# A diffusion step on one core: the norm chains ranked 300 instructions further up in the planner's order

## The chip, the core and the metric

The kernel runs on one core of a Trainium2 chip. The core has five engines, each with its own queue that it works off strictly in order: TensorE (PE, whose weight loads the profile lists as PEld), VectorE (DVE), ScalarE (ACT), GpSimd (POOL) and SyncE (SP, which issues most transfers here). An instruction that waits holds up everything behind it in its own queue. The metric is device time in microseconds (us) of one execution; the kernel before is told by the median of 3 runs.

## The reference, cut to what matters

Two layers run over 1024 latent and 128 context tokens of width 1024. Each layer is

```
h = rmsnorm(x) * g * (1 + scale1) + shift1
x = x + gate1 * (concat(diff_attn(h), fourier(h), mla(h), gqa(h)) @ w_out)
h = rmsnorm(x) * g * (1 + scale2) + shift2
x = x + gate2 * (square(relu(h @ w1)) @ w2)
```

and the end is `y = rmsnorm(x) * g`, with `rmsnorm(x) = x * rsqrt(mean(x*x) + 1e-6)` over the 1024 channels of a token. So every token is normalised five times: before the mixer and before the MLP of each layer, and at the end.

## The kernel before, in words

Activations lie transposed: 8 tiles of 128 channels by 1152 tokens, and the tokens are worked in three blocks b = 0, 1, 2 of 384 (block 2 holds the last 256 latent and the 128 context tokens). One norm of one block therefore is: square each of 8 tiles on ACT (L531), add them up to one tile `acc` on POOL or DVE (L534, function `sq_add`), and then `norm_scale`. With five norms and three blocks it is called 15 times.

`norm_scale` (L538) is the chain that the change touches. **Sums:** three products of `acc` with a column of ones give the sum of squares of 3 x 128 tokens in a PSUM tile of the pool `psA` (six PE instructions `psA<-ones,pg`, as a float32 product is two). **Chain:** a DVE copy to SBUF (L548, `ss<-psA`), then `rstd`: DVE multiply and add (L323, `rv`), ACT square root (L327, `rs`), DVE reciprocal (L328, `ry`), and four DVE steps of one Newton iteration (L330, L333, L335, L338; the last writes `ro`). Each of these works on 128 x 3 elements. **Spread:** three products of `ro`, broadcast along a row, with the identity put 1/rms of each token on all 128 partitions, again in a `psA` tile (six PE instructions `psA<-ident,ro`). `psA` has two buffers.

The spread is then read by the tiles' multiplications on DVE: in `norm_h` (the norm before a mixer, L567 in layer 0, L570 in layer 1), in `norm_mlp` (L2003), and in `final` (L1958, followed by the store of the tile). In `norm_mlp` ACT then applies scale and shift (L2005), ACT writes the float16 high part (L306) and POOL, or DVE for one in four, the low part (L303); these parts feed the MLP's products, of which the first chunk (function `plain`) needs block 0, 1 and 2 in turn. In `norm_h` DVE writes the high part (L578) and DVE or POOL the low part (L303). DVE also adds every product of the output projection and of the MLP to x (L1685).

The order of the work has two makers. The program is written as Python generators, and `run` advances them in turn by weights; that gives each instruction its place in the program. Inside `norm_scale` one `yield PACE` between chain and spread lets another generator take a step in between. A planner then orders each engine's queue before the run: it plays the program through a model of the chip, and an engine that comes free takes, of the instructions whose inputs are ready in the model, the one of lowest rank. The rank is the place in the program; inside `with self.pri(n)` (which is `tc.high_priority(offset=n)`) the rank is n less. Before the change this is used for the output tiles of the attention (`YO_PRI`, 40) and for L1685 (`RE_PRI`, 60). The queue order is fixed by this plan, whatever the chip's real times are.

Of the kernel before, what the change touches and what calls it, by code (L numbers as in the profile page):

```python
# [21 lines left out]
D = 1024  # L22
# [48 lines left out]
P_NORM = 1  # L71
Y_ROT = 2

YO_PRI, RE_PRI = 40, 60

WL_DVE = (1, 1, 1)
XL_DVE = (0, 1, 2, 3)
# [126 lines left out]
class Kern:  # L204
# [334 lines left out]
    def norm_scale(self, b):  # L539

        nc = self.nc
        acc = self.acc.pop(b)
        p = self.ps("A")
        for j in range(3):
            self.mm(p[:, j:j + 1], acc[:, 128 * j:128 * j + 128], self.ones, True, True)
        self.free(acc)
        ss = self.sm([128, 3], "ss")
        nc.vector.tensor_copy(ss, p[:, 0:3])  # L548
        r = self.rstd(ss, 3, 1.0 / D)
        for _ in range(P_NORM):  # L550
            yield PACE
        pb = self.ps("A")
        for j in range(3):
            self.mm(pb[:, 128 * j:128 * j + 128], r[:, j:j + 1].to_broadcast([128, 128]), self.ident, True, True)
        return pb

    def norm_h(self, l, i, x, b, h, own=False):
# [1733 lines left out]
```

## Time and profile before

| | |
|---|---|
| median of 3 runs (lowest, highest) | 3426.4 us (3425.98, 3429.53) |
| profiled execution, its time | 3424.58 us |
| its span (first to last instruction) | 3422.5 us |
| busy PE, PEld | 3102.8 us (91%), 2225.8 us (65%) |
| busy DVE, ACT, POOL | 2271.7 (66%), 1594.7 (47%), 1453.2 us (42%) |
| chain that ended last, by engine | PE 58%, DVE 17%, DMA 8%, POOL 6%, issue 5%, ACT 5% |
| mean granted TensorE clock | 0.945 of 2.4 GHz |

A busy share is of the whole span. The stretches between the long phases matter here: output projection to MLP (about 940 to 1060 us in layer 0, 2615 to 2700 us in layer 1), MLP of layer 0 to mixer of layer 1 (1725 to 1800 us), and the end (3385 to 3422 us). In a row of the timeline, `[3.56 <-DVE ro L338]` says that the engine sat idle for 3.56 us before the row and that the end of that DVE instruction released it.

### The profile page before, as it was taken

The page shows a single profiled execution, that of the slowest core. Times are in us where ns is not written, and L with a number is a line of the kernel's source. Part 1 is how long each engine was busy: PE and PEld are TensorE (multiplying, and loading weights), DVE is VectorE, ACT ScalarE, POOL GpSimd, SP SyncE. Part 2 cuts the span into 40 slices and gives each one's busy share as a digit, 9 for nine tenths or more (in the row PEclk, how much of TensorE's full clock was granted, in tenths as well). Part 3 has the DMA queues.
Part 4 walks back from the last instruction along what each step waited for, and adds up shares of the span by engine and source line. Part 5 has one row for each costly group of instructions (what it writes and reads, how often), then busy time and mean ns, then how long its engine had stood idle before and what let it go on. Part 6 is the DMA issues. An engine that isn't in the chain of part 4 may idle for free.

```text
span 3422.5 us, 60243 instructions
## 1 busy us (share of the span) xinstructions
PE 3102.8 (91%) x23658; PEld 2225.8 (65%) x23658; DVE 2271.7 (66%) x5215; ACT 1594.7 (47%) x2594; POOL 1453.2 (42%) x1140
## 2 busy tenths in 40 slices
PE   7998788899978999999989978889999799999997
PEld 5887566677954555555578866667789455555554
DVE  6864565655387777777696565665444687777776
ACT  4432565667264334443343326567653544344432
POOL 1331366767454223232263226678654523222222
PEclk8999798999989999999999988899999899999998
DMA  6642444333312111111036433332341111111101
GB/s 221 200 153 84 125 152 153 97 97 103 114 38 74 43 33 62 42 46 50 15 136 200 143 93 124 128 114 71 108 157 44 50 44 44 49 47 47 50 25 56
DMA packets 140549, 310.86 MB, mean 91 GB/s; under 512 B 16613, under 2 KB 85682, under 8 KB 140266
## 3 DMA queue, kind: packets, MB, share of 16 engines
q1 hardware_dynamic: 134858, 300.85, 27.1%
q10 hardware_dynamic: 5408, 6.18, 0.5%
q8 instruction: 185, 3.03, 0.4%
q14 instruction: 98, 0.80, 0.1%
HBM read 233.87 MB, written 72.82 MB: 90 GB/s over the span
## 4 chain that ended last, share of the span: by engine, by line
PE 58%; DVE 17%; DMA 8%; POOL 6%; issue 5%; ACT 5%; SPq 0%; ACTq 0%; DVEq 0%; POOLq 0%
PE psD L281 38%; PE psA L281 9%; PE psB L281 6%; DVE pg L303 5%; POOL pg L303 5%; PE psC L281 4%; DMA pg<-in_ada_p 3%; DVE pg L1685 2%; DMA pg<-mqr 2%; ACT pg L306 2%; DVE mx L1327 1%; DMA pg<-in_dft_lat 1%; ACT pg L1819 1%; DVE wm L1745 1%; ACT pg L1822 1%
## 5 line engine op out<-in xcount | busy, mean ns | idle before, releaser
L281 PE MATMUL psD<-pg,pg 128*128 128x384 f16 (+6 forms) x10510 | 2029.7, 341 | 76.2 <-DVE pg L303 25.4
L303 POOL TENSOR_TENSOR pg<-pg,pg 128x1024 f16<-128x1024 f32 (+8 forms) x743 | 1190.3, 1616 | 1124.9 <-ACT pg L306 413.4
L281 PEld LDWEIGHTS <-pg 128*128 128x128 f16 x16056 | 1084.9, 100 | 771.8 <-issue 120.5
L303 DVE TENSOR_TENSOR pg<-pg,pg 128x512 f16<-128x512 f32 (+11 forms) x617 | 477.8, 795 | 265.0 <-ACT pg L306 249.8
L281 PEld LDWEIGHTS psD<-pg,pg 128*128 128x128 f32 x3576 | 613.2, 194 | 39.9 <-DVE pg L303 16.1
L306 ACT ACTIVATE pg<-pg 128x512 f16<-128x512 f32 (+8 forms) x777 | 431.2, 588 | 345.8 <-POOL pg L303 78.3
L281 PE MATMUL psA<-pg,pg 128*128 128x128 f16 (+7 forms) x2752 | 505.3, 295 | 87.4 <-DVE mx L1327 30.3
L1685 DVE SCALAR_TENSOR_TENSOR pg<-psD,gc,pg 128x384 f32<-128x384 f32 (+2 forms) x1024 | 473.4, 505 | 13.5 <-PE psD L281 13.3
L1327 DVE TENSOR_REDUCE mx<-psA 128x1 f32<-128x384 f32 x512 | 281.6, 555 | 212.9 <-PE psA L281 199.6
L1373 ACT ACTIVATE pg<-psB 128x1024 f32<-128x1024 f32 x320 | 301.5, 945 | 253.1 <-PE psB L281 219.7
L281 PEld LDWEIGHTS psA<-pg,pg 96*128 96x128 f32 (+2 forms) x1377 | 256.2, 209 | 149.4 <-DVE mx L1327 46.3
L281 PE MATMUL psB<-pg,pg 97*128 97x512 f32 (+3 forms) x1064 | 332.1, 428 | 18.3 <-ACT pg L1373 13.5
L281 PE MATMUL psC<-pg,pg 128*128 128x65 f16 (+1 forms) x7008 | 332.1, 201 | 9.7 <-POOL pg L303 8.2
L1380 ACT ACTIVATE pg<-pg 128x1024 f16<-128x1024 f32 x320 | 308.3, 980 | 35.8 <-DMA pg<-mk 13.8
L281 PEld LDWEIGHTS psB<-pg,pg 97*128 97x128 f32 (+3 forms) x1064 | 203.2, 207 | 50.8 <-ACT pg L1373 16.1
L281 PE MATMUL psD<-pg 128*128 128x384 f16 (+1 forms) x674 | 219.7, 328 | 8.3 <-DVE pg L303 4.8
L1332 DVE TENSOR_REDUCE mx<-psA 128x1 f32<-128x384 f32 x256 | 142.2, 556 | 100.4 <-PE psA L281 87.9
L1770 ACT ACTIVATE pg<-pg,wm 128x1024 f32<-128x1024 f32 x32 | 36.7, 1148 | 356.3 <-DVE wm L2042 356.1
L1785 POOL TENSOR_TENSOR pg<-pg 128x512 f32<-128x512 f32 x32 | 43.4, 1356 | 233.4 <-PE psA L281 181.6
L1751 POOL PARTITION_ALL_REDUCE wm<-wm x32 | 11.9, 373 | 277.7 <-DVE wm L1705 235.0
L531 ACT ACTIVATE pg<-pg 128x384 f32<-128x384 f32 x120 | 61.1, 520 | 143.1 <-DVE pg L1685 131.0
L306 ACT ACTIVATE pg<-psD 128x384 f32<-128x384 f32 (+3 forms) x104 | 54.4, 529 | 137.2 <-PE psD L281 132.1
(205 smaller groups left out, 2153.9 us busy)
## 6 DMA issues: line engine op xcount, KB each, us to landing
pg<-in_mlp_w SPq DMA_DIRECT2D x128, 512.0 KB
pg<-in_ada_p SPq DMA_DIRECT2D x96, 512.0 KB
pg<-in_w_out SPq DMA_DIRECT2D x16, 512.0 KB
pg<-y_dram SPq DMA_DIRECT2D x42, 192.0 KB
pg<-sk SPq DMA_DIRECT2D x16, 436.5 KB
sqp<-pg SPq DMA_DIRECT2D x36, 192.0 KB
mqp<-pg SPq DMA_DIRECT2D x36, 192.0 KB
pg<-sqp SPq DMA_DIRECT2D x16, 432.0 KB
```

Source lines behind the costliest of these rows:

```text
L281: self.nc.tensor.matmul(out, lhsT=lhsT, rhs=rhs, start=start, stop=stop, skip_group_check=skip)
L303: eng.tensor_tensor(out, a, b, ALU.subtract)
L306: self.nc.scalar.activation(out, in_, AF.Copy)
L531: self.nc.scalar.activation(q.t, x, AF.Square)
L1327: nc.vector.reduce_max(mx[:, t, i:i + 1], p[:, 0:TB], axis=AX.X)
L1332: nc.vector.reduce_max(mx[:, t, 2:3], p[:, 128:512], axis=AX.X)
L1373: nc.scalar.activation(e[:, 0:n], src, AF.Exp, scale=M["scale"])
L1380: nc.scalar.activation(pp[:, 0, 0:n], e[:, 0:n], AF.Copy)
L1685: self.nc.vector.scalar_tensor_tensor(xs, o(p), g, xs, op0=ALU.mult, op1=ALU.add)
L1745: nc.vector.reduce_max(m[:, i:i + 1], s[i].t, axis=AX.XY, apply_absolute_value=True)
L1770: nc.scalar.activation(v.t, v.t, AF.Identity, scale=sc)
L1785: nc.gpsimd.tensor_tensor(s1.t, a21, a22, ALU.add)
```

## The change

`norm_scale` wraps its sums with the chain, and then its spread, in `with self.pri(NRM_PRI)`, with `NRM_PRI = 300`. Nothing is computed in another way, no instruction is added or removed, and the place of every other instruction in the program stays. The multiplications that read the spread keep their rank.

```diff
-YO_PRI, RE_PRI = 40, 60
+YO_PRI, RE_PRI, NRM_PRI = 40, 60, 300
...
         acc = self.acc.pop(b)
-        p = self.ps("A")
-        for j in range(3):
-            self.mm(p[:, j:j + 1], acc[:, 128 * j:128 * j + 128], self.ones, True, True)
-        self.free(acc)
-        ss = self.sm([128, 3], "ss")
-        nc.vector.tensor_copy(ss, p[:, 0:3])
-        r = self.rstd(ss, 3, 1.0 / D)
+        with self.pri(NRM_PRI):
+            p = self.ps("A")
+            for j in range(3):
+                self.mm(p[:, j:j + 1], acc[:, 128 * j:128 * j + 128], self.ones, True, True)
+            self.free(acc)
+            ss = self.sm([128, 3], "ss")
+            nc.vector.tensor_copy(ss, p[:, 0:3])
+            r = self.rstd(ss, 3, 1.0 / D)
         for _ in range(P_NORM):
             yield PACE
-        pb = self.ps("A")
-        for j in range(3):
-            self.mm(pb[:, 128 * j:128 * j + 128], r[:, j:j + 1].to_broadcast([128, 128]), self.ident, True, True)
+        with self.pri(NRM_PRI):
+            pb = self.ps("A")
+            for j in range(3):
+                self.mm(pb[:, 128 * j:128 * j + 128], r[:, j:j + 1].to_broadcast([128, 128]), self.ident, True, True)
         return pb
```

## Rows read from the trace of the kernel before

**Rows 1.** Groups by line and form, whole span: busy, mean ns | idle before, releasers.
```profile
L281 PE MATMUL psA<-ident,ro 128*128 128x128 f32 x90 | 16.8, 335 | 25.5 <-DVE ro L338 15.5 <-DVE wm L1721 10.1
L281 PE MATMUL psA<-ones,pg 128*128 128x1 f32 x90 | 13.7, 268 | 10.0 <-DVE pg L534 5.1 <-POOL pg L534 4.9
```
**Rows 2.** Timeline, final norm of blocks 1 and 2: start, length, engine, line [idle].
```profile
3396.88 0.72 PE L281 MATMUL psA<-ones,pg 128*128 128x1 f32 x6
...
3403.35 0.15 DVE L548 COPY ss<-psA 128x3 f32<-128x3 f32 x1
3403.49 2.06 POOL L534 TENSOR_TENSOR pg<-pg,pg 128x384 f32<-128x384 f32 x2 [0.18 <-ACT pg L531]
...
3406.08 1.65 PE L281 MATMUL psA<-ident,ro 128*128 128x128 f32 x6 [4.55 <-DVE ro L338]
3407.52 1.28 PE L281 MATMUL psA<-ones,pg 128*128 128x1 f32 x6
...
3411.98 0.15 DVE L548 COPY ss<-psA 128x3 f32<-128x3 f32 x1
...
3413.51 1.62 PE L281 MATMUL psA<-ident,ro 128*128 128x128 f32 x6 [4.71 <-DVE ro L338]
3415.24 4.29 DVE L1958 SCALAR_TENSOR_TENSOR pg<-pg,cols,psA 128x384 f32<-128x384 f32 x8 [1.87 <-PE psA L281]
```
**Rows 3.** Timeline, layer 0's MLP norm, block 2 (and the end of block 1's).
```profile
976.29 0.73 PE L281 MATMUL psA<-ones,pg 128*128 128x1 f32 x6
...
977.87 3.32 DVE L2003 TENSOR_TENSOR pg<-pg,psA 128x384 f32<-128x384 f32 x7
...
981.11 0.15 DVE L548 COPY ss<-psA 128x3 f32<-128x3 f32 x1
...
992.11 0.19 ACT L327 ACTIVATE rs<-rv 128x3 f32<-128x3 f32 x1
...
993.40 1.62 PE L281 MATMUL psA<-ident,ro 128*128 128x128 f32 x6 [10.05 <-DVE wm L1721]
```
**Rows 4.** Timeline of POOL in the same stretch.
```profile
989.84 0.37 POOL L1751 PARTITION_ALL_REDUCE wm<-wm  x1 [6.11 <-DVE pg L303]
996.90 12.66 POOL L303 TENSOR_TENSOR pg<-pg,pg 128x384 f16<-128x384 f32 x17 [6.69 <-ACT pg L2005]
```
**Rows 5.** Windows: stretch, length, busy PE, PEld, DVE, ACT, POOL, clock, DMA share, GB/s.
```profile
997.00:1021.00 24.00, 14.64 (x85) 8.52 (x85) 21.14 (x38) 13.12 (x47) 23.86 (x35) 0.83 0.00 1
...
1725.00:1755.00 30.00, 24.99 (x144) 18.47 (x144) 27.98 (x62) 13.58 (x26) 20.13 (x19) 0.96 0.54 177
1755.00:1790.00 35.00, 28.68 (x144) 27.46 (x145) 32.18 (x60) 16.33 (x33) 19.35 (x18) 0.89 0.14 47
```
**Rows 6.** Timeline, layer 1's MLP norm, block 2.
```profile
2653.72 0.52 ACT L306 ACTIVATE pg<-pg 128x384 f16<-128x384 f32 x1 [0.49 <-DVE pg L303]
...
2657.30 0.52 ACT L306 ACTIVATE pg<-pg 128x384 f16<-128x384 f32 x1 [1.03 <-DVE pg L303]
...
2666.35 0.60 ACT L2005 ACTIVATE pg<-pg,hg 128x256 f32<-128x256 f32 x1 [2.00 <-DVE pg L2003]
...
2680.75 9.00 POOL L303 TENSOR_TENSOR pg<-pg,pg 128x128 f16<-128x128 f32 x7 [0.86 <-ACT pg L306]
...
2683.39 2.22 DVE L303 TENSOR_TENSOR pg<-pg,pg 128x512 f32<-128x512 f32 x4
...
2687.15 0.37 PE L281 MATMUL psD<-pg,pg 128*128 128x128 f16 x2 [4.81 <-POOL pg L303]
```
**Rows 7.** Timeline, layer 1's first norm, blocks 1 and 2.
```profile
1753.28 1.65 PE L281 MATMUL psA<-ident,ro 128*128 128x128 f32 x6 [3.56 <-DVE ro L338]
...
1754.96 1.48 DVE L570 TENSOR_TENSOR pg<-pg,psA 128x384 f32<-128x384 f32 x3 [1.47 <-PE psA L281]
...
1769.29 1.95 DVE L570 TENSOR_TENSOR pg<-pg,psA 128x384 f32<-128x384 f32 x4 [1.09 <-PE psA L281]
```
**Rows 8.** Timeline, layer 0's MLP norm, block 0: PE waits for the sums.
```profile
942.06 1.44 PE L281 MATMUL psA<-ones,pg 128*128 128x1 f32 x6 [3.77 <-POOL pg L534]
```

## The prediction

> **What bounds the kernel now.** I read the page first: PE is busy nine tenths of the span and leads the chain that ended last, so a norm can cost time only where PE has run out of other work. Then the groups by line and form, for the two PE steps that frame each chain. All 15 spreads together were preceded by 25.5 us of idle PE and all 15 sums by 10.0 us [rows 1]. That is all that PE itself loses to the norms, and an outer bound of the direct gain. The 10.0 us are waits for the adds that make `acc`; the change doesn't touch those. The 10.1 us put down to `wm` L1721 are one wait at a spread like the others; that instruction merely ended last.
>
> The timeline then tells which norms these are. In eight of the fifteen (the first two of layer 0's first norm, blocks 0 and 1 of both MLP norms, block 0 of layer 1's first norm and of the final one) PE does other products between sums and spread and never stops. The others are all of block 1 or 2, where few products are left. Where the wait is long, an order makes it long: in layer 0's MLP norm of block 2 the sums end at 977.0, but the copy starts at 981.1, right after a run of block 1's multiplications, and the square root starts only at 992.1, behind block 1's work on ACT [rows 3]. With nothing ahead the steps are quick: in the last norm of all, copy to spread is 3411.98 to 3413.51, 1.53 us [rows 2].
>
> Last, the windows, for what takes over when a chain is no longer late. That decides the sum, because a wait that ends earlier is worth nothing where another one ends at the old time.
>
> **The change part by part.** No instruction comes or goes. Each chain's eight small steps (seven on DVE, the square root on ACT) go ahead of work that was ranked before them by up to 300 places; that covers a whole block's tiles, so I take it that the chain follows its sums at once. What it passes on DVE and ACT is late by the steps' own length, some 1.5 us in all, and is not on PE's path in the same norm. On SP nothing moves: the chain issues no transfer, and the stores behind the final norm follow L1958. An early spread also holds one of the two `psA` buffers longer; the other users nearby, layer 1's rotary products, come after the last of these spreads, so I price that at nothing.
>
> The end. The last add ends at 3403.49 + 2.06 = 3405.55 [rows 2]. Today the last sums start 1.97 us later, because on PE they stand behind block 1's spread, which waited 4.55 us for its chain (sums done at 3397.6, copy at 3403.35). Then the copy waits until 3411.98 for eight multiplications of block 1. With both chains first: sums 3405.6 to 3406.9 (1.28), copy to spread 1.53, spread 1.62, and eight multiplications 4.29, with about 0.1 us at two handovers: 3414.5. Today they end at 3415.24 + 4.29 = 3419.5. Block 1's own eight (the same 4.29 us) fit into the 5 us of DVE that are free between 3403.5 and 3410.2 while PE and ACT work. Stores follow the multiplications as today. Gain 5.0 us. Below it is 3.5, if block 1's chain delays the last additions to x by its 1.5 us; above it nothing more is there.
>
> Layer 1's MLP norm, block 2. PE hardly waits at this spread, but ACT has to run all of block 2's scaling and high parts after it and does so without a pause from 2666.35 on. Before that it stood idle for 0.49, 1.03 and 2.00 us [rows 6], and these gaps are what early data can fill: 3.5 us. Bounds: 0 where the planner puts the pieces elsewhere, and 3.5 + 4.81 = 8.3 if the POOL wait at 2687.15 goes too [rows 6].
>
> On this wait a rule can be weighed. Seven low parts took 9.00 us on POOL, 1.29 us each, in a stretch in which DVE ran subtractions of two SBUF tiles without a break [rows 6]. The Trainium skill, SBUF — State Buffer, section "Who interferes with whom", says that a DVE instruction with two SBUF inputs and a GpSimd one that reads SBUF exclude each other, and that the later one stands for the whole of the other. By that rule the burst and the low parts, which follow from the same data, would move together and the 4.81 us stay; without it they might go and the sum would be 15.9 instead of 11.1 us.
>
> Layer 1's first norm, blocks 1 and 2. DVE is busy 27.98 of 30 and 32.18 of 35 us there [rows 5], and its work stays the same. What an early spread can give back is DVE's own pause between a chain and the first multiplication: 1.47 and 1.09 us [rows 7], 2.6 in all. Bounds: 0, and the 3.56 us that PE stood at the first of the two spreads, since PE waits for DVE later anyway.
>
> Layer 0's MLP norm, block 2. Here PE loses the most, 10.05 us [rows 3], and I count it as nothing. After the spread PE needs the low parts of block 1, and POOL starts on them only at 996.90, after a stretch around the all-reduce with 6.11 and 6.69 us of idle time [rows 4]. It is then busy for 23.86 of 24 us [rows 5]. A spread at 980 instead of 993 leaves POOL's start and its work where they are. Bounds: 0 and 10.05.
>
> Everything else: 0. The eight norms without a wait keep their cover, other products on PE. If that cover failed, the nearest row for a wait at the head of PE's queue is the 3.77 us before layer 0's first MLP sums [rows 8]; that is the bound below nothing for each of them. The third block of the very first norm has a share in the 25.5 us under 2 us, with DVE busy throughout: 0.
>
> Sum: 5.0 + 3.5 + 2.6 = 11.1 us, 3424.6 - 11.1 = 3413.5 for the profiled execution. The median of the runs is 1.8 us above that execution, so 3426.4 - 11.1 = **3415.3 us**.
>
> **The rivals.** *More comes back.* POOL's order around the all-reduce changes with the plan and the two largest waits go too: 11.1 + 10.05 + 4.81 = 26.0, 3400 us. For it: the plan is made anew, and PE is idle there. Against it: POOL's full window. *Only the end.* The engines behind the chains (POOL, ACT, DVE) swallow the rest: 3426.4 - 5.0 = 3421.4. For it: in all three places another engine has little slack. *Nothing.* The copies stand late because the planner's model has the sums late, not because of rank: 3426. Against it: copies start just behind runs of lower-ranked multiplications, in the end twice [rows 2, 3]. *Slower.* The spread enters PE's queue as soon as the model has `ro` ready. Where real DVE is behind the model, PE stands at the spread, with ready products behind it. Price: 3.77 us per place [rows 8] at the eight norms that show no wait today, 30.2 us; with the gain, 3426.4 + 30.2 - 11.1 = 3445.5. From three such waits on (11.3 us) the gain is gone; five make it measurably slower. For it: PE already stood at sums that the plan took for ready [rows 8]. Against it: a chain without anything ahead is 1.53 us [rows 2], far shorter than the products that PE has in hand in those norms.
>
> **How the numbers follow.** My forecast, a gain between 7 and 18 us, 0.46; more, 0.14; only the end, 0.21; nothing, 0.08; slower, 0.11. A measurement of this kernel can tell 0.2%, 6.9 us, from no change, so faster is 0.46 + 0.14 = 0.60, within 0.2% 0.29, slower 0.11. The range leaves out the tails of the first and last rival: 3400 (all upper bounds of the three places, about) to 3428. The forecast's own range is 3408 to 3420.
>
> **What would show it.** Right: all fifteen copies start within a microsecond or so of the end of their sums; copy to spread falls to under 4 us in the norms named, most of all from 12 us in layer 0's; the last eight multiplications start about 4.7 us after the last add (today 9.7); idle time before the spreads falls from 25.5 us to a few, while the waits for POOL's low parts in layer 0's transition grow by about as much. Wrong: PE waiting for `ro` in norms that have no wait now; an all-reduce at another place of POOL's queue; a copy still behind a run of multiplications; or a total off by more than the sum of the places named, which would mean that the new plan moved work far from the norms.

## The result and the profile after

The changed kernel takes 3444.2 us in the median of 4 runs (3442.0 to 3445.9), the kernel before 3426.2 us in the same comparison: 1.0052 of it, 95% interval 1.0037 to 1.0067. Repeated in five rounds it gave 1.0052 again (1.0040 to 1.0065). So the change costs about 18 us, where 11 us of gain were forecast. The profiled execution of after has a span of 3440.2 us and a mean granted clock of 0.944 (0.945 before).

First the groups by line and form of after, which answer to [rows 1]; the last row is the copy that starts the chain (4.7 us of idle DVE before it in the kernel before).

```profile
L281 PE MATMUL psA<-ident,ro 128*128 128x128 f32 x90 | 16.0, 322 | 10.8 <-DVE ro L338 10.8
L281 PE MATMUL psA<-ones,pg 128*128 128x1 f32 x90 | 13.1, 261 | 25.3 <-POOL pg L534 20.4 <-DVE pg L534 4.9
L549 DVE COPY ss<-psA 128x3 f32<-128x3 f32 x15 | 2.4, 160 | 21.6 <-PE psA L281 21.6
```

The chain did what was forecast: idle PE before the spreads fell from 25.5 to 10.8 us. But what left the spreads came back in front of the sums, 10.0 to 25.3 us, all of the growth in waits for POOL's last add. Eight of the fifteen sums have a new or a longer wait.

The final norm's timeline (start, length, engine, line, [idle]) answers to [rows 2].

```profile
3403.42 0.83 PE L281 MATMUL psA<-ones,pg 128*128 128x1 f32 x6 [2.03 <-POOL pg L534]
...
3404.29 0.16 DVE L549 COPY ss<-psA 128x3 f32<-128x3 f32 x1 [2.89 <-PE psA L281]
...
3404.64 0.62 DVE L1687 SCALAR_TENSOR_TENSOR pg<-psD,gc,pg 128x384 f32<-128x384 f32 x1
...
3405.89 2.06 POOL L534 TENSOR_TENSOR pg<-pg 128x384 f32<-128x384 f32 x2 [2.52 <-ACT pg L531]
...
3415.14 0.83 PE L281 MATMUL psA<-ones,pg 128*128 128x1 f32 x6 [1.07 <-POOL pg L534]
...
3426.41 0.83 PE L281 MATMUL psA<-ones,pg 128*128 128x1 f32 x6 [2.83 <-POOL pg L534]
3427.28 0.16 DVE L549 COPY ss<-psA 128x3 f32<-128x3 f32 x1 [1.34 <-PE psA L281]
...
3430.62 1.62 PE L281 MATMUL psA<-ident,ro 128*128 128x128 f32 x6 [3.38 <-DVE ro L338]
3432.35 4.29 DVE L1960 SCALAR_TENSOR_TENSOR pg<-pg,cols,psA 128x384 f32<-128x384 f32 x8 [1.88 <-PE psA L281]
```

Every copy now follows its sums at once, but the sums themselves start late: PE stands at each of the three until POOL has added the last square. DVE in turn stands at the copy, and POOL stands idle for 2.52 us between two adds, because the additions to x (L1687) that feed them come late. From the first sums to the last instruction it takes 36.8 us (34.7 before).

The largest loss is in layer 1's first norm. The windows before and after, between the same PE instructions (columns as in [rows 5]), and PE's waits in about the same stretch of before and then of after (total, times, longest):

```profile
1700.00:1880.00 180.00, 162.66 (x944) 142.53 (x942) 138.98 (x311) 79.12 (x175) 82.75 (x75) 0.96 0.48 159
```
```profile
1708.50:1896.10 187.60, 164.41 (x944) 142.80 (x941) 136.31 (x311) 79.36 (x175) 82.73 (x75) 0.95 0.46 153
```
```profile
PE psA L281 <- DVE ro L338: 4.4, 2, 3.6
...
PE psA L281 <- POOL pg L534: 0.5, 1, 0.5
```
```profile
PE psA L281 <- POOL pg L534: 6.3, 3, 2.9
...
PE psA L281 <- DVE ro L338: 3.0, 1, 3.0
```

The stretch is 7.6 us longer with the same 944 PE instructions, and 5.8 us of that is more idle PE. The spreads gave back 1.4 us, the sums took 5.8. How it comes about is in the timeline of POOL's adds and PE's sums, before and then after:

```profile
1719.09 5.31 POOL L534 TENSOR_TENSOR pg<-pg,pg 128x384 f32<-128x384 f32 x5 [0.37 <-ACT pg L531]
...
1724.45 0.83 PE L281 MATMUL psA<-ones,pg 128*128 128x1 f32 x6 [0.50 <-POOL pg L534]
...
1733.61 0.72 PE L281 MATMUL psA<-ones,pg 128*128 128x1 f32 x6
```
```profile
1727.54 5.30 POOL L534 TENSOR_TENSOR pg<-pg,pg 128x384 f32<-128x384 f32 x5 [0.37 <-ACT pg L531]
...
1732.89 0.83 PE L281 MATMUL psA<-ones,pg 128*128 128x1 f32 x6 [2.78 <-POOL pg L534]
...
1735.36 0.99 POOL L534 TENSOR_TENSOR pg<-pg 128x384 f32<-128x384 f32 x1 [2.52 <-ACT pg L531]
...
1746.99 0.83 PE L281 MATMUL psA<-ones,pg 128*128 128x1 f32 x6 [2.94 <-POOL pg L534]
```

POOL's last five adds run back to back at 1.06 us each, in both kernels. In the kernel before, 14 products of the next block stand in PE's queue just ahead of block 0's sums, and they last until the adds are done but for 0.50 us. In after the sums stand in front of those 14 products. PE waits 2.78 us with ready work behind it; the next block's products, additions, squares and adds are late in turn (POOL idle 2.52 us), and block 1's sums, 9.2 us after block 0's before, come 14.1 us after them. The wait at block 0's sums is only a part of this delay; another part comes with the raised spread, as the experiments show.

Layer 0's MLP norm, block 2, answers to [rows 3 and 4]: PE and the chain, then POOL.

```profile
986.07 0.73 PE L281 MATMUL psA<-ones,pg 128*128 128x1 f32 x6
...
987.00 0.15 DVE L549 COPY ss<-psA 128x3 f32<-128x3 f32 x1
...
988.34 0.19 ACT L327 ACTIVATE rs<-rv 128x3 f32<-128x3 f32 x1
...
991.37 0.83 PE L281 MATMUL psA<-ident,ro 128*128 128x128 f32 x6
```
```profile
990.59 9.85 POOL L303 TENSOR_TENSOR pg<-pg,pg 128x1024 f16<-128x1024 f32 x7 [5.80 <-ACT pg L306]
...
1009.52 0.37 POOL L1753 PARTITION_ALL_REDUCE wm<-wm  x1 [5.93 <-DVE pg L303]
1017.04 8.36 POOL L303 TENSOR_TENSOR pg<-pg,pg 128x384 f16<-128x384 f32 x16 [7.15 <-ACT pg L306]
```

PE comes to this stretch 9.4 us later than before, so the spread is 11.4 us earlier against it. The chain takes 4.4 us instead of 12.3 and the 10.05 us at the spread are gone. Yet the place as a whole is only 1.2 us shorter. POOL's all-reduce has moved behind block 1's first low parts, with its 5.93 and 7.15 us of idle POOL, and PE's waits from 940 to 1060 us now are these:

```profile
PE psD L281 <- POOL pg L303: 7.7, 4, 3.2
PE psD L281 <- ACT pg L306: 6.9, 4, 3.8
PE psA L281 <- POOL pg L534: 5.5, 2, 3.5
PE psD L281 <- DVE pg L1687: 3.9, 3, 2.8
```

In the 120 us of before that answer to these, POOL's low parts cost 10.9 us, ACT's high parts 1.9, the sums 3.8 and the additions to x 1.6. The last three grew by 9.0 us together and the first fell by 3.2: most of the ten us is waited elsewhere.

Layer 1's MLP norm, against [rows 6]:

```profile
2648.66 1.19 PE L281 MATMUL psA<-ones,pg 128*128 128x1 f32 x6 [2.01 <-POOL pg L534]
...
2663.48 0.73 PE L281 MATMUL psA<-ones,pg 128*128 128x1 f32 x6
...
2671.32 0.91 PE L281 MATMUL psA<-ident,ro 128*128 128x128 f32 x6 [2.87 <-DVE ro L338]
```

PE comes to this place 12.5 us later than before. Against that, block 1's sums stand 4.8 us earlier than before, with 40 products behind them that were ahead of them, and PE waits 2.01 us there. Block 2's last add ends 5.8 us later, its sums come 4.1 us later, and PE waits at its spread too (2.87 us, 0.24 before).

### The profile page after: what moved, and what is told of

It reads as the page before. It is cut to its first block, busy times and chain, and to the rows that moved or that the text cites. A ratio compares the mean times of both kernels' runs of the same rounds, so it can differ in the third digit from the quotient of the medians.

```text
span 3440.2 us, 60254 instructions
## 1 busy us (share of the span) xinstructions
PE 3113.2 (90%) x23658; PEld 2229.0 (65%) x23658; DVE 2282.9 (66%) x5215; ACT 1595.3 (46%) x2594; POOL 1449.4 (42%) x1140
## 4 chain that ended last, share of the span: by engine, by line
PE 55%; DVE 18%; DMA 9%; POOL 6%; issue 5%; ACT 5%; SPq 1%; ACTq 0%; POOLq 0%; DVEq 0%
PE psD L281 36%; PE psA L281 9%; DVE pg L303 6%; PE psB L281 5%; POOL pg L303 4%; PE psC L281 4%; DVE pg L1687 3%; DMA pg<-in_ada_p 3%; DMA pg<-mqr 2%; ACT pg L306 2%; DVE mx L1329 1%; DMA pg<-in_dft_lat 1%; DVE wm L1747 1%; ACT pg L1821 1%; POOL pg L534 1%
## 5 line engine op out<-in xcount | busy, mean ns | idle before, releaser
L303 DVE TENSOR_TENSOR pg<-pg,pg 128x512 f16<-128x512 f32 (+12 forms) x617 | 475.1, 792 | 253.7 <-ACT pg L306 240.4
L306 ACT ACTIVATE pg<-pg 128x512 f16<-128x512 f32 (+9 forms) x777 | 431.1, 589 | 354.7 <-DVE pg L303 77.6
L281 PE MATMUL psA<-pg,pg 128*128 128x128 f16 (+7 forms) x2752 | 506.7, 296 | 82.6 <-DVE mx L1329 27.7
L1687 DVE SCALAR_TENSOR_TENSOR pg<-psD,gc,pg 128x384 f32<-128x384 f32 (+2 forms) x1024 | 475.6, 508 | 12.6 <-PE psD L281 12.3
L281 PE MATMUL psB<-pg,pg 97*128 97x512 f32 (+3 forms) x1064 | 331.2, 428 | 19.1 <-ACT pg L1375 14.3
L1382 ACT ACTIVATE pg<-pg 128x1024 f16<-128x1024 f32 x320 | 308.2, 980 | 35.5 <-DMA pg<-mk 16.3
L281 PE MATMUL psD<-pg 128*128 128x384 f16 (+2 forms) x674 | 219.8, 328 | 12.2 <-DVE pg L1687 7.2
L1772 ACT ACTIVATE pg<-pg,wm 128x1024 f32<-128x1024 f32 x32 | 36.8, 1149 | 359.1 <-DVE wm L2044 359.0
```

The costliest lines, as they stand in the source:

```text
L281: self.nc.tensor.matmul(out, lhsT=lhsT, rhs=rhs, start=start, stop=stop, skip_group_check=skip)
L303: eng.tensor_tensor(out, a, b, ALU.subtract)
L306: self.nc.scalar.activation(out, in_, AF.Copy)
L1382: nc.scalar.activation(pp[:, 0, 0:n], e[:, 0:n], AF.Copy)
L1687: self.nc.vector.scalar_tensor_tensor(xs, o(p), g, xs, op0=ALU.mult, op1=ALU.add)
L1772: nc.scalar.activation(v.t, v.t, AF.Identity, scale=sc)
```

## The experiments

Each ratio is against the kernel before in the same five rounds on the same chip (three chips in all), with its 95% interval. It is not the ratio of the medians that the text quotes, and differs from that by up to 0.11%. The idle times (us) are the totals of one profile each. "Sums", "chain" and "spread" are the parts ranked 300 further up.

| kernel | ratio | idle PE before sums | before spreads | idle DVE before copies |
|---|---|---|---|---|
| before | 1 | 10.0 | 25.5 | 4.7 |
| the change (repeated) | 1.0052 (1.0040 to 1.0065) | 25.2 | 10.8 | 22.1 |
| sums | 1.0042 (1.0025 to 1.0059) | 20.3 | 25.9 | 19.7 |
| chain | 0.9988 (0.9973 to 1.0003) | 15.2 | 12.7 | 8.9 |
| spread | 1.0000 (0.9987 to 1.0013) | 10.3 | 27.7 | 4.1 |
| chain, spread | 0.9994 (0.9981 to 1.0007) | 14.5 | 13.0 | 9.6 |
| sums, chain | 1.0033 (1.0022 to 1.0045) | 23.8 | 12.0 | 22.0 |
| change, additions to x at 400 | 1.0037 (1.0025 to 1.0048) | 22.6 | 9.8 | 19.7 |
| change, squares and adds at 300 | 1.0022 (1.0010 to 1.0034) | 22.7 | 10.5 | 20.4 |
| chain, spread; sums up 20 | 1.0006 (0.9991 to 1.0020) | 20.0 | 14.0 | 10.2 |
| chain, spread; sums down 20 | 0.9978 (0.9968 to 0.9988) | 8.9 | 18.5 | 8.4 |
| chain, spread; sums down 80 | **0.9950** (0.9937 to 0.9962) | 6.9 | 11.0 | 6.3 |
| sums down 80 alone | 1.0008 (0.9997 to 1.0020) | 6.2 | 19.7 | 3.8 |
| change in the final norm only | 0.9999 (0.9986 to 1.0012) | 16.3 | 21.6 | 10.6 |
| change in layer 0's first norm only | 1.0001 (0.9986 to 1.0015) | 10.0 | 24.4 | 4.9 |
| change in one block of one norm | 1.0020 (1.0010 to 1.0030) | 12.3 | 26.6 | 7.7 |

**Sums alone.** The sums keep `with self.pri(NRM_PRI)`, chain and spread lose it.

```diff
         with self.pri(NRM_PRI):
             p = self.ps("A")
...
             self.free(acc)
-            ss = self.sm([128, 3], "ss")
-            nc.vector.tensor_copy(ss, p[:, 0:3])
-            r = self.rstd(ss, 3, 1.0 / D)
+        ss = self.sm([128, 3], "ss")
+        nc.vector.tensor_copy(ss, p[:, 0:3])
+        r = self.rstd(ss, 3, 1.0 / D)
```

> Only the sums are ranked 300 further up; chain and spread keep their rank. The planner's order of layer 0's first norm is then that of the kernel before, and the other four norms change. Theory A (the sums reach the head of PE's queue before the adds are done on the chip, and PE stands there): idle PE before the sums rises from 10.0 us to between 20 and 27 us (25.3 in the changed kernel), with little or nothing back before the spreads (25.5 us before), so the time is 3426 + 10 to 18 = 3436 to 3444 us. Theory B (the raised chain does the harm: its copy stands at the head of DVE's queue, with ready additions to x behind it): without a raised chain the sums cost little, idle before sums under 14 us, time within 4 us of 3426. Theory C (the new order of layer 0's first norm and what follows from it cost most of the 18 us): nothing in the first 900 us, time within 5 us of 3426.

3437.1 us, and as A has it; its two groups:

```profile
L281 PE MATMUL psA<-ident,ro 128*128 128x128 f32 x90 | 17.4, 332 | 25.9 <-DVE ro L338 16.0 <-DVE wm L1722 9.9
L281 PE MATMUL psA<-ones,pg 128*128 128x1 f32 x90 | 14.6, 278 | 20.3 <-POOL pg L534 15.5 <-DVE pg L534 4.8
```

B and C fall as the main cause: no chain was raised and layer 0's first norm has the old order. DVE stood at the copies for 19.7 us although they were not raised, so that idle time follows from the late sums. Read place by place, as in the table further below, the sums alone lose 4.0 us in layer 0's MLP norm, 2.5 and 6.0 in layer 1's two norms and 5.1 at the end.

**Chain alone.** Only `ss`, copy and `rstd` stand in `with self.pri(NRM_PRI)`.

```diff
-        with self.pri(NRM_PRI):
-            p = self.ps("A")
...
+        p = self.ps("A")
...
+        with self.pri(NRM_PRI):
             ss = self.sm([128, 3], "ss")
```

> Only the chain from the copy to ro is ranked 300 further up; sums and spread keep their rank. PE's order at the end is that of the kernel before. Theory A: idle PE before the sums stays near 10 us, idle before the spreads falls from 25.5 us to 12 or so, and the kernel is faster than before: 3413 to 3422 us. Theory B: the copies wait on DVE as in the changed kernel (idle before them 21.6 us there, 4.7 before), additions to x and with them the adds come late, idle before the sums rises to 20 us or more, time 3434 to 3444. Theory C: layer 0's first norm has the changed order here too, so 3431 to 3440 whatever the waits do.

3421.5 us, in A's range; the interval just reaches no change. The waits:

```profile
L281 PE MATMUL psA<-ident,ro 128*128 128x128 f32 x90 | 14.5, 302 | 12.7 <-DVE ro L338 12.7
L281 PE MATMUL psA<-ones,pg 128*128 128x1 f32 x90 | 12.8, 258 | 15.2 <-POOL pg L534 10.1 <-DVE pg L534 5.0
```

12.8 us go from the spreads and 5.2 come back at the sums, 4.4 of them at the very last ones: PE has nothing left to do there and waits for POOL's last add instead.

```profile
3406.57 1.44 PE L281 MATMUL psA<-ones,pg 128*128 128x1 f32 x6 [4.36 <-POOL pg L534]
...
3411.39 1.62 PE L281 MATMUL psA<-ident,ro 128*128 128x128 f32 x6 [3.39 <-DVE ro L338]
```

**The change in the final norm alone, and in layer 0's first norm alone.** A counter `nn` of the norms chooses 12, 13, 14 or 0, 1, 2.

```diff
+        n = NRM_PRI if self.nn in (12, 13, 14) else 0
+        self.nn += 1
-        with self.pri(NRM_PRI):
+        with self.pri(n):
```

> The change in the final norm alone (its three blocks); all orders up to there are those of the kernel before. Theories A and B: the end alone loses what it lost in the changed kernel, from the first sums of the final norm to the last instruction 36.8 us against 34.7 before, that is 2 to 3 us: 3428 to 3430 us, PE waiting 1 to 3 us before each of the three sums on POOL's last add. Theory C: the end by itself gains, as the prediction had it, 3421 us. The stretch up to 3375 us also shows how far two executions of the same order drift apart: the changed kernel was 4.4 us later between 600 and 900 us and 3.5 us earlier between 2150 and 2600 us, where no engine's order differs, and if that is drift, this run shows drifts of that size against the profile of before as well.

> The change in layer 0's first norm alone. Theories A and B: no PE wait came or went there, so at most what its new order of the rotary products does: PE's shift at 300 us under 2 us, time within 5 us of 3426. Theory C: the shift of 4.5 us at 300 us comes back and grows to 8 to 10 us by 900 us: 3434 to 3437 us.

Neither moves the whole time. The end alone takes 36.5 us from its first sums on against 34.7, a loss of 1.8 us, a little under what A expected, with the same three waits at the sums as in after (2.02, 1.07 and 2.83 us). C falls: with layer 0's first norm changed PE's shift is 2.7 us at 300 us, a little over A's bound, and 0.0 at 900. Both also show the drift, which is told below.

**Chain and spread; sums and chain; spread alone.** The same edit for other parts; the cut shows the spread alone, against the change.

```diff
-        with self.pri(NRM_PRI):
-            p = self.ps("A")
+        p = self.ps("A")
...
         with self.pri(NRM_PRI):
             pb = self.ps("A")
```

> Chain and spread are ranked 300 further up, the sums keep their rank. Sums alone cost 10.7 us and the chain alone gave back 4.9, so of the changed kernel's 18 us some 12 are not accounted for by adding the two. Theory S (the raised spread is the rest: it holds a buffer of psA or stands at the head of PE's queue): 3421.5 + 12 = 3430 to 3437 us, with PE waiting for ro in norms that had no such wait. Theory I (sums and chain raised together are the rest: the copy stands at the head of DVE's queue as soon as the sums are in PE's, and additions to x wait behind it; the spread costs nothing): 3417 to 3425 us, idle before the spreads 8 to 13 us, before the sums 10 to 16 us.

> Sums and chain are ranked 300 further up, the spread keeps its rank. Theory I: the changed kernel's whole loss without its spread, 3440 to 3447 us, idle before the sums 22 to 28 us. Theory S: the sum of the two parts alone, 3426 + 10.7 - 4.9 = 3432 us, between 3428 and 3436.

> The spread alone is ranked 300 further up. Theory S: slower by about 12 us, 3434 to 3442 us. Theory I: no change that can be told, 3422 to 3430 us; idle before the spreads stays between 20 and 27 us, since the chain that feeds it is as late as before.

Chain and spread came to 3425.4 us, just above I's range and well below S's, and the spread alone changes nothing. Sums and chain came to 3437.4 us, below I's range and just above S's: near the sum of the two alone (0.42 - 0.12 = 0.30%, measured 0.33%). All three raised, 0.52%, is some 6 us more than that; the intervals just overlap.

The profiles show where a spread costs once the sums are raised too. In layer 1's first norm, sums and chain lose 4.0 us and all three lose 7.5 and 8.0. There the raised spread puts block 0's spread ahead of block 1's products on PE, and block 0's multiplications, scaling and high parts then go in between block 1's additions, squares and adds. From the start of block 0's sums to the end of block 1's last add it takes 7.7 us before, 10.6 with the spread alone, 11.5 with the sums alone, 11.4 with sums and chain, and 14.0 with all three. So PE waits 0.91 us at block 1's sums with sums and chain, and 2.94 us with the spread as well:

```profile
1735.00 0.83 PE L281 MATMUL psA<-ones,pg 128*128 128x1 f32 x6 [2.80 <-POOL pg L534]
...
1746.42 0.83 PE L281 MATMUL psA<-ones,pg 128*128 128x1 f32 x6 [0.91 <-POOL pg L534]
```

These are the rows with sums and chain; those of the change stand above.

**Additions to x first.** `RE_PRI` from 60 to 400, the rest as in the change.

```diff
-YO_PRI, RE_PRI, NRM_PRI = 40, 60, 300
+YO_PRI, RE_PRI, NRM_PRI = 40, 400, 300
```

> The change as it is, and DVE's additions to x ranked 400 instead of 60 further up, so that they go ahead of copy and chain in the planner's choice. Theory I: the blocked additions were the rest, so the loss shrinks to that of the sums alone or less: 3430 to 3438 us, and the last adds of block 1 and 2 of the norms come earlier again (in layer 1's first norm block 1's ended at 1746.9 us, 14.0 after block 0's sums; before it was 7.7). Theory S: DVE's order among these doesn't matter, 3440 to 3448 us. In both PE goes on waiting for POOL's last add before the sums, since the sums still go first in PE's queue when the model has them ready.

3439.7 us, between the two, and I's marker failed: block 1's last add in layer 1's first norm still ends 14.0 us after block 0's sums. So in that norm the copy ahead of the additions is not what delays them; the sums alone (11.5 us) and sums with the chain (11.4 us) say the same. In layer 1's MLP norm the rank of the additions has a share: block 2's last add ends 2.6 us earlier than with the change, and that place takes 1.0 us less than in the profile of before, where the change takes 2.9 and 3.4 us more.

**The sums further down or a little up.** The sums get a rank of their own; chain and spread stay at 300.

```diff
-        with self.pri(NRM_PRI):
+        with self.pri(-20):
             p = self.ps("A")
...
+        with self.pri(NRM_PRI):
             ss = self.sm([128, 3], "ss")
```

> Chain and spread ranked 300 further up, the sums 20 further down than their place. So far idle PE before the sums was 20 to 25 us in every kernel with the sums raised and 10 to 15 us in those without. Theory A (the plan has the adds done earlier than the chip, so the sums wait wherever they stand close behind them): the wait falls below the 14.5 us that the same kernel has with the sums at their own rank, to 5 to 10 us, and the time is 3415 to 3423 us. Theory D (there is no trend in it; each rank is another order and the raised one is merely a bad one): idle before the sums and the time follow no line, 3422 to 3436 us.

> As the last, with the sums 80 further down. Theory A: the wait before the sums falls to under 6 us (only layer 0's first norm, 4.8 us, keeps it), but the chain starts later where the sums did not wait, so that idle PE before the spreads grows again from 13 us to 15 to 25: 3417 to 3430 us. Theory D: as for the last, 3422 to 3440 us.

> Chain and spread ranked 300 further up, the sums 20 further up. Theory A: 20 places already pass the products that stood between the adds and the sums, so most of the loss is there: idle before the sums 17 to 24 us, 3431 to 3440 us. Theory D: anything between 3420 and 3445 us.

The trend is A's: with the sums at +20, 0, -20 and -80 the times are 1.0006, 0.9994, 0.9978 and 0.9950, the idle time before them 20.0, 14.5, 8.9 and 6.9 us. The intervals of the first two times overlap; -20 and -80 stand clear of each other. Two misses. Down 80 was better than I expected, 3411.7 us, 16 us under the kernel before, because the chains did not get late (11.0 us before the spreads):

```profile
L281 PE MATMUL psA<-ident,ro 128*128 128x128 f32 x90 | 17.3, 343 | 11.0 <-DVE ro L338 7.9 <-DVE wm L1756 3.1
L281 PE MATMUL psA<-ones,pg 128*128 128x1 f32 x90 | 13.1, 250 | 6.9 <-DVE pg L534 4.4 <-POOL pg L534 2.5
```

And up 20 had the waits expected, 20.0 us, but not the time (3427.2 us): a wait at the sums doesn't cost its own length everywhere. In the three middle norms it puts the sums of block 0 or 1 ahead of 8 to 18 products, the full change ahead of 13 to 40.

**Squares and adds raised too.** In `sq_add` everything stands in `with self.pri(NRM_PRI)`, the rest as in the change.

```diff
-        self.nc.scalar.activation(q.t, x, AF.Square)
+        with self.pri(NRM_PRI):
+            self.nc.scalar.activation(q.t, x, AF.Square)
...
```

> The change, and the squares on ACT and the adds on POOL and DVE that make acc ranked 300 further up as well. Theory A: the adds are late on the chip because what they wait for comes late (POOL stood idle before them), not because of their rank; idle before the sums stays between 18 and 27 us and the time is 3435 to 3446 us. Theory R (the adds are late because other work on ACT and POOL goes ahead of them, while the sums were put before theirs): idle before the sums falls to 10 to 14 us and the time to 3432 us or less.

3438.6 us with 22.7 us before the sums: both as A has it. But 1.0022 (1.0010 to 1.0034) is clear of the change's 1.0052, so the rank of the adds has a share. It lies mainly in layer 1's MLP norm: block 1's last add ends 5.1 us earlier than with the change, PE's wait at those sums falls from 2.01 to 0.16 us, and the place takes 3.4 us less than in the profile of before, as it does in kernels that leave it alone. In layer 1's first norm and the final one all waits of 1 us or more at the sums stay within 0.1 us: there the adds are not late because of their rank.

**Sums down alone.** As sums down 80, without the raised chain and spread.

> The sums 80 further down, chain and spread at their own rank. Theory A1 (the late sums are the whole gain of the kernel with sums down and chain up, since PE never stands at them): as fast as that, 3408 to 3416 us. Theory A2 (both are needed: the sums out of the way of ready products, and the chain ahead of the multiplications, so that the later sums don't make later spreads): about half of its 16 us at most, idle PE before the spreads 25 us or more, 3418 to 3430 us.

```profile
L281 PE MATMUL psA<-ident,ro 128*128 128x128 f32 x90 | 16.7, 333 | 19.7 <-DVE ro L338 19.7
L281 PE MATMUL psA<-ones,pg 128*128 128x1 f32 x90 | 13.5, 252 | 6.2 <-DVE pg L534 4.9 <-POOL pg L534 1.3
```

No gain (1.0008): A2 holds, though fewer waits were left at the spreads than it expected. Both are needed.

**The change again, and the change in one block.** The second takes the counter above with `(6,)`, block 0 of layer 1's first norm.

> The changed kernel once more, in the same rounds as the others, for an interval as narrow as theirs and a second profile. Sums raised together with other parts gave 1.0022 to 1.0042 of the time before; the changed kernel gave 1.0052 from 4 executions. All theories: 1.003 to 1.0055. In the profile, if the steps between 600 and 900 us and between 2150 and 2600 us were drift, they come out otherwise this time, while layer 1's first norm again loses 5 to 9 us and PE again stands 20 to 27 us before the sums.

> The change in one of the fifteen norms: block 0 of layer 1's first norm, whose sums move 28 places up in PE's queue, in front of 14 products with their weight loads. Theory F (the wait at one block's sums is passed on: the products behind it feed the next block's sum of squares, which is late in turn): PE stands 2 to 3 us before block 0's sums (0.5 before), and block 1's last add ends 3 to 10 us later against block 0's sums than the 7.7 us of before; from 1715 to 1880 us the run loses 2 to 6 us. Theory G (each block pays only at its own sums): block 1's last add stays within 2 us of before, and the stretch loses 0 to 2.5 us. The whole time can't tell them apart: within 0.2% of before.

The repeat: 25.2 us before the sums, layer 1's first norm 8.0 us longer. Of the two steps, the one between 2150 and 2600 us shrank from 4.1 to 1.3 us, and the one between 600 and 900 us came again (3.8 and 3.9 us). That this one is drift rests on the other runs, in whose profiles with unchanged order there it is 3.4, -0.2 and 0.3 us. One block's rank alone costs 1.0020. PE in it:

```profile
1729.26 0.83 PE L282 MATMUL psA<-ones,pg 128*128 128x1 f32 x6 [2.85 <-POOL pg L535]
...
1743.37 0.83 PE L282 MATMUL psA<-ones,pg 128*128 128x1 f32 x6 [0.84 <-POOL pg L535]
```

PE waits 2.85 us at block 0's sums. Block 1's sums, of unchanged rank and place, come 14.1 us after them instead of 9.2, and have to wait too. The stretch is 5.9 us longer. F holds: the delay is passed on to the next block. It doesn't all come through the sums, as this block's spread is raised too: block 1's last add ends 14.0 us after block 0's sums, as in the change, and 11.5 us with the sums alone.

## Why the prediction was wrong

**The step that failed** is "The 10.0 us are waits for the adds that make `acc`; the change doesn't touch those." The change ranks the sums up as well as the chain. That moved nine of the fifteen ahead of 10 to 40 PE products, each with its weight load, and among these were the products that had covered POOL's serial adds. Seven of the nine and the very last of all wait longer, and the 10.0 us became 25.3. "The eight norms without a wait keep their cover" was asked of the spreads only, where it held, and not of the sums.

**The sign was that of the "slower" rival**, which had 0.11. Its mechanism was right in kind (PE at the head of its queue, the plan ahead of the chip, ready products behind), but it put the wait at the spreads of the eight norms without one, which wait 0.57 us in all in after. The wait stands at the sums. That its time came so close (3445.5 forecast, 3444.2 measured) is luck: it is 30.2 us of waits at those spreads less 11.1 us of gain, and neither came. The whole costs more than the idle time in front of sums and spreads, which together hardly changed (35.5 to 36.1 us): the next block's delay shows at other instructions.

**Place by place**, by how much longer PE takes than in the profile of before from one product to another, the same two in every profile (those that start at 75 and 300, 930 and 1100, 1718 and 1875, 2605 and 2850 us in the profile of before, and from 3375 us to the end), less the mean of the runs with the change elsewhere only (the end, the first norm, one block):

| place | forecast | the change, both profiles | unchanged orders | difference |
|---|---|---|---|---|
| layer 0, first norm | 0 | +5.4, +1.5 | +0.4, +0.7 | +2.9 |
| layer 0, MLP norm | 0 | -1.2, -1.5 | +0.9, -1.5, -0.3 | -1.0 |
| layer 1, first norm | -2.6 | +7.5, +8.0 | 0.0, +0.6 | +7.4 |
| layer 1, MLP norm | -3.5 | +2.9, +3.4 | -3.7, -3.5, -2.9 | +6.5 |
| the end | -5.0 | +2.0, +1.7 | 0.0, 0.0 | +1.8 |

The sum is 17.6 us, of the 18 measured. In layer 0's first norm no wait of its sums or spreads grew. Yet the ten profiles with its new order took 0.4 to 5.4 us more there (2.6 in the mean), the five later ones with its old order -0.6 to +0.7 (0.3). What costs these 2 us is open.

- *The end, -5.0.* Mis-sized twice even for the chain alone, where it gained 1.3 us. Copy to spread takes 3.35 us, not 1.53, because the plan puts block 1's multiplications between the chain's steps; and the last add ends 19.5 us after the norm's first sums, not 17.7.
- *Layer 1's first norm, -2.6.* The chain alone gave -2.4: right. The sums, and with them the spread, turned it.
- *Layer 1's MLP norm, -3.5.* Mis-sized. The chain alone gave -4.3, of which unchanged orders show 3.4 as well: 0.9 are left. The bound of 8.3 with its 4.81 us rested on a wait that other executions of the same order don't have (below).
- *Layer 0's MLP norm, 0 because POOL is full.* Right in size by luck, for another reason: the all-reduce moved, and POOL was busy 14.3 of 24 us (10 us further on, with the shift) instead of 23.9. With the sums down 80 the all-reduce comes at 983.97 and the place gains 8.8 us, most of the upper bound I gave.
- *The early spread, 0 (buffers of `psA`).* Right for the spread alone, 1.0000. With the sums raised it is not free: 3.5 to 4.0 us in layer 1's first norm, through what it puts ahead of the next block's adds.
- *What would show it.* Copies at once after the sums: all fifteen. Copy to spread under 4 us in the six norms named: three (3.35, 3.74 and 3.97 us; the others 4.4, 6.7 and 7.1). The last eight multiplications 4.7 us after the last add: 6.0 us. Idle time before spreads to a few: to 10.8. PE waiting for `ro` where it hardly had: 2.9 us instead of 0.2 in layer 1's MLP norm, 0.6 in the final one's block 0. More waiting for POOL's low parts in layer 0's transition: less, 7.7 us instead of 10.9. An all-reduce elsewhere: yes. "The new plan moved work far from the norms": no; the engines' orders differ in the five norms and what overlaps them, nowhere else.

## What to carry to other kernels

In a queue planned by a model, the rank of an instruction that ends a serial chain on a slower engine decides what covers the rest of that chain. What worked here: raise what follows the wait, and push the waiting instruction itself down behind work that is ready. Before raising a group, ask of each part what now stands behind it in its queue. Here the same edit split in two, chain and spread up and sums down 80, turned 18 us of loss into 16 of gain, and neither half alone gave a gain that its interval tells from none. How far down is best is open: 20 and 80 places were tried, and nothing beyond.

## What the runs showed of the hardware

**An instruction on POOL that sometimes takes 5.96 us.** The 9.00 us for seven low parts in [rows 6] are one of 5.96 us, five of 0.42 and one larger tile of 1.15; the 1.29 us each of the prediction is a mean over these.

```profile
2681.14 5.96 POOL L303 TENSOR_TENSOR pg<-pg,pg 128x128 f16<-128x128 f32 x1
```

In the run with the change in the final norm only, whose order there is that of before, the same work reads:

```profile
2678.19 6.05 POOL L304 TENSOR_TENSOR pg<-pg,pg 128x128 f16<-128x128 f32 x13 [0.89 <-ACT pg L307]
```

That is 0.47 us each, with no 4.81 us wait of PE, and its layer 1 MLP norm is 3.7 us shorter. Of 17 profiles three have the 5.96 us. The slow one of before ended at 2687.10, 0.29 us after a run of eleven subtractions on DVE without a break, which had begun 0.04 us after it. The Trainium skill, SBUF — State Buffer, section "Who interferes with whom", has the one stand for the whole of the other's instruction; here it outlasted that whole run, of instructions of 0.28 to 0.68 us each. That this hits the same queue order in some executions only is what these runs add; why is open.

**Drift.** Between 320 and 895 us the 16 later profiles took -4.7 to +6.7 us more than before, between 1900 and 2570 us -7.1 to +5.7. Among them are the three with the change elsewhere only (-2.6 to +4.1 and -5.6 to -2.9), whose queues there are those of before; the same kernel before ran from 3414 to 3438 us. Layer 1's MLP from 2860 to 3375 us repeated within 0.3 us. The granted clock there was 1.00 (of 2.4 GHz) in all 17 profiles. In the first of the two drifting stretches its mean was 0.877 to 0.895: 0.877 in the slowest profile, 0.895 in the fastest. Whether the clock makes the drift or follows from PE's idle time is not shown. A few us between two single executions mean nothing unless they are read place by place.
